# Stick-breaking sums in two reduced-precision passes with split operands instead of plain fp32 products

## The chip, the core and the metric

The program runs on one core of one Trainium2 chip. Its engines work side by side, each through its own queue in program order: TensorE (PE in the rows, PEld for its weight loads), VectorE (DVE), ScalarE (ACT), GpSimd (POOL) and SyncE (SP, which issues most DMAs). The metric is the time of one execution in device microseconds; less is better.

## The reference, cut to what matters

Two transformer-like blocks follow one another on 512 frames of width 1024. The change sits in one of the three mixers of the first block, a causal attention whose weights come from breaking a stick:

```
def stick_breaking_attention(q, k, v):        # 4 heads, head size 64, blocks of 128 frames
    for o in range(n):                        # nearest key block first
        z = einsum('bhnqd,bhnkd->bhnqk', qb[:, :, o:], kb[:, :, :n - o])
        log_rest = log_sigmoid(-z)            # diagonal block: masked
        after = einsum('bhnqj,js->bhnqs', log_rest, after_mat) + carry[:, :, o:, :, None]
        w = exp(log_sigmoid(z) + after)
        out = out.at[:, :, o:].add(einsum('bhnqk,bhnkd->bhnqd', w, vb[:, :, :n - o]))
        carry = carry.at[:, :, o:].add(sum(log_rest, axis=-1))
```

Beside it stand a chunked attention with relative positions (8 heads) and a short convolution. The three results are normalised in groups, multiplied by `w_out` and added to `x`; a feed-forward layer and the whole second block come after that.

## The kernel before

Everything is held transposed: 128 partitions by 512 frames. Large products run with both operands split in a high and a low part of the type fp32r, as three passes (`mm3`: low by high, high by low, high by high). The small products inside the attentions are plain fp32.

`block1` (line 606) issues the projections of the first block unit by unit. A unit is one 128x1024 slice of weights, w0, w1, ..., split into `w..h` on ACT and `w..l` on DVE; one projection takes eight groups of three passes. The order is the string `SEQ1`. The units that matter here are w16 to w19 (`qkb`, queries and keys of the last two pairs of chunked heads) and w20 to w23 (`g`, the convolution gates). Then comes the output projection `wo`: its first three row blocks (units w24 to w26) are gathered in the order `PRE1`, which is first the normalised output `ys0`, then `ys3, ys4, ys1, ys2`, then `ys6`, then `ys5, ys7`.

Beside this main stream run generators, in lanes of a merger (class `Merge`, line 138): the four stick-breaking heads (`sb_head`, lane `sb`, three at a time), the chunked heads (`ch_head`, lane `at`, four at a time), the convolution (`cv`) and small statistics (`ln`). When the program is built, the merger keeps a clock for each engine (`Clock`, line 64: a cost for each instruction and a time at which each tile will be ready). A generator yields the time from which it wants to go on; its next step is put in front of the next main product only when the planned time of PE has passed that time. Each engine then runs the instructions in the order in which they were written. So the table of costs and the yielded times set the order on all queues. Where `block1` asks for an output `ys[k]` that no generator has made yet, the merger runs side steps until it is there, with no main product between them.

One head of `sb_head` goes through the key blocks 3, 2, 1, 0; a block takes n = 128, 256, 384, 512 query columns. For each: a score product `z` on PE; `ab` (Abs, Exp, Ln) on ACT; `sp` (the softplus) on DVE; a triangular select on POOL; the product of the triangle `ntri` with `sp`, added into `z`; from the second block on the product of `nones` with the carried sum, n - 128 columns wide; then `w` = Exp on ACT, a select on POOL, and on DVE the new carry. At its end `osb` gathers the head's output, the group norm follows (`gsq` on ACT, `gst` on DVE and a power on POOL), and after each second head four transposes (`yT`) and a split into `ys..h` and `ys..l`. `ys1` needs head 3, and head 3 enters the lane when the first of heads 0 to 2 has left it.

One chunked head takes four blocks in turn: scores `sc`, `s` on DVE and ACT, its maximum `m` on DVE, Exp on ACT, transposes `pt`, a copy `pT`, the product `och` with the values, and a scaling on DVE (`sm`, `y`).

All calls go through the helper at line 134, so nearly every row of the profile carries that line; tiles tell the places apart.

Of the kernel before, what the change touches and what calls it, by code (L numbers as in the profile page):

```python
# [10 lines left out]
F32 = mybir.dt.float32  # L11
F32R = mybir.dt.float32r
# [3 lines left out]
AF = mybir.ActivationFunctionType  # L16
ALU = mybir.AluOpType
# [4 lines left out]
P = 128  # L22
T = 512
# [40 lines left out]
class Clock:  # L64
# [43 lines left out]
    def at(self, *aps):  # L108

        t = 0.0  # L110
        for x in aps:
            r = self.ready.get(x.tensor.name)
            if r:
                lo, hi = self.span(x)
                t = max([t] + [e[2] for e in r if e[0] < hi and e[1] > lo])
        return t
# [74 lines left out]
def body(tc, a):  # L191
    nc = tc.nc
    clk = Clock()
    V, S, G, PE = (Engine(clk, k, e) for k, e in (("V", nc.vector), ("S", nc.scalar), ("G", nc.gpsimd),
                                                  ("PE", nc.tensor)))
    at, room = clk.at, clk.room
    with ExitStack() as ctx:
        ctx.enter_context(tc.manual_schedule())

        def mkpool(stack, name, **k):  # L200
            return stack.enter_context(tc.tile_pool(name=name, bufs=1, **k))
# [25 lines left out]
        nones = cst.tile([P, P], F32, name="nones")  # L227
# [7 lines left out]
        ntri = cst.tile([P, P], F32, name="ntri")  # L235
# [7 lines left out]
        raws, parts = {}, {}  # L243
# [75 lines left out]
        wk = mkpool(ph, "wk")  # L319
# [4 lines left out]
        def t2(name, dt=F32):  # L324
            return wk.tile([P, T], dt, tag="t2", name=name, bufs=NT2)
# [73 lines left out]


        preload("natural_log_exp_and_others")
        mg = Merge(clk, at=4, sb=3, ln=1, cv=1, cg=1, ls=1, rw=1)
        run = mg.run
        y_tok = [t2(f"y{k}").rearrange("p (b d) -> p b d", b=NB) for k in range(KT)]
# [2 lines left out]
        def group_norm(*gs):  # L407

            st_ = []
            for g in gs:  # L410
                yg = y_tok[g // 2][:, :, (g % 2) * 64:(g % 2) * 64 + 64]
                sq = t2(f"gsq{g}")[:, :NB * 64].rearrange("p (b d) -> p b d", b=NB)
                S.activation(sq, yg, AF.Square)
                s_ = wk.tile([P, 3, NB], F32, tag="gst", name=f"gst{g}", bufs=6)
                st_.append((yg, sq, s_))
            yield at(*(x[1] for x in st_))
            for yg, sq, s_ in st_:
                V.tensor_reduce(s_[:, 0], sq, axis=AX.X, op=ALU.add)
                V.tensor_scalar(s_[:, 1], s_[:, 0], 1.0 / 64, EPS, ALU.mult, ALU.add)
                G.tensor_tensor(s_[:, 2], s_[:, 1], half[:, :NB], ALU.pow)  # L420
            yield at(*(x[2] for x in st_))
            for yg, sq, s_ in st_:
                V.tensor_tensor(yg, yg, s_[:, 2][:, :, None].to_broadcast([P, NB, 64]), ALU.mult)

        def y_transpose(k):
            pt = psd(f"yT{k}")
            for b in range(NB):
                PE.transpose(pt[:, b * P:(b + 1) * P], y_tok[k][:, b, :], ident)
            ys[k] = split(pt, f"ys{k}", scale=pc("out_norm", k))
# [3 lines left out]
        def sb_head(h):  # L433
            q, k = Q[f"qa{h // 2}"], Q[f"ka{h // 2}"]
            rows = slice((h % 2) * 64, (h % 2) * 64 + 64)
            wts = {}
            carry = None
            for kb in (3, 2, 1, 0):
                c0 = kb * P
                n = T - c0  # L440
                z = psd(f"z{h}{kb}")
                zz = z[:, c0:]
                PE.matmul(zz, k[rows, c0:c0 + P], q[rows, c0:], start=True, stop=True)
                ab = t2(f"ab{h}{kb}")
                S.activation(ab[:, c0:], zz, AF.Abs)
                S.activation(ab[:, c0:], ab[:, c0:], AF.Exp, scale=-1.0)
                S.activation(ab[:, c0:], ab[:, c0:], AF.Ln, bias=1.0)
                yield at(ab)
                sp = t2(f"sp{h}{kb}")
                V.scalar_tensor_tensor(sp[:, c0:], zz, 0.0, ab[:, c0:], ALU.max, ALU.add)  # L450

                G.affine_select(sp[:, c0:c0 + P], sp[:, c0:c0 + P], pattern=[[1, P]], base=0,
                                channel_multiplier=-1, compare_op=ALU.is_gt, fill=0.0)
                yield at(sp)
                PE.matmul(zz, ntri, sp[:, c0:], start=False, stop=True, skip_group_check=True)
                if carry is not None:
                    PE.matmul(z[:, c0 + P:], nones, carry[:, c0 + P:], start=False, stop=True,
                              skip_group_check=True)
                w = t2(f"w{h}{kb}")
                S.activation(w[:, c0:], zz, AF.Exp)  # L460
                G.affine_select(w[:, c0:c0 + P], w[:, c0:c0 + P], pattern=[[1, P]], base=0,
                                channel_multiplier=-1, compare_op=ALU.is_gt, fill=0.0)
                wts[kb] = w
                if kb:
                    if carry is not None:
                        V.tensor_tensor(sp[:, c0 + P:], sp[:, c0 + P:], carry[:, c0 + P:], ALU.add)
                    carry = sp
                yield None if kb else at(*wts.values())
            o = psd(f"osb{h}")
            for qb in range(NB):  # L470
                for kb in range(qb + 1):
                    PE.matmul(o[:, qb * 64:(qb + 1) * 64], wts[kb][:, qb * P:(qb + 1) * P],
                              va[kb // 2][:, kb % 2, h * 64:(h + 1) * 64], start=kb == 0, stop=kb == qb)
            V.tensor_copy(y_tok[h // 2][:, :, (h % 2) * 64:(h % 2) * 64 + 64],
                          o[:, :256].rearrange("p (b d) -> p b d", b=NB))
            yield at(y_tok[h // 2])
            yield from group_norm(h)
            if h % 2:
                yield at(y_tok[h // 2])
                y_transpose(h // 2)  # L480
# [125 lines left out]
        def block1():  # L606
# [3 lines left out]
            for x in SEQ1:  # L610
                if x == "a":
# [9 lines left out]
                    for h in range(4):  # L621
                        mg.spawn("sb", sb_head(h))
# [137 lines left out]
        for g in range(2):  # L760
            c = 64 * g
# [256 lines left out]
        wk = mkpool(ph, "wk2")  # L1018
# [523 lines left out]
```

## Time and profile before

| | us |
|---|---|
| median of three runs | 2438.34 (2435.8 to 2440.07) |
| profiled execution, device time | 2441.93 |
| its span, first to last instruction | 2440.1 |
| PE busy in the span | 2369.1 (97%) |
| DVE, ACT, POOL busy | 1759.5, 1036.5, 741.1 |

The span is read as one long stream of matmuls: PE is busy 97% of it. A busy PE need not be PE at its peak, since matmuls are pipelined and their ends are modelled; the starts of consecutive matmuls tell what one costs. The stick-breaking heads live between 132 and 250 us.

### The profile page before, as it was taken

To read this page: it belongs to the slowest core of one execution; us is meant where nothing else is said; L and a number is where in the kernel's file an instruction comes from. 1 tells how busy PE (TensorE), PEld (TensorE's weight loads), DVE (VectorE), ACT (ScalarE), POOL (GpSimd) and SP (SyncE) were. 2 spreads that over 40 slices of the span, in tenths; PEclk is the share of its full clock that TensorE was granted. 3 is DMA by queue.
4 is the path that set the end of the run, shared out by engine and by line. 5 is a ranking of instruction groups with operands and counts; after the bars stand their busy time and mean duration, and the time that the engine had idled before them with its cause. 6 is when DMAs were issued, how large, how long until landed. Compare 5 with 4: busy or idle time off the path is not lost.

```text
span 2440.1 us, 33936 instructions
## 1 busy us (share of the span) xinstructions
PE 2369.1 (97%) x13121; PEld 2113.9 (87%) x13121; DVE 1759.5 (72%) x3167; ACT 1036.5 (42%) x1557; POOL 741.1 (30%) x590
## 2 busy tenths in 40 slices
PE   9999999999999899999999999999998999999997
PEld 7777888888776667778889999999997999999997
DVE  4636644443357779755789899899997888888874
ACT  4454332222246456544334343455554333333333
POOL 2122011110116668401234455333322332323211
PEclk9999999999999999999999999999999999999998
DMA  4111222232211112222224788899998999999972
GB/s 169 59 53 35 89 88 104 86 104 89 93 61 64 58 53 69 88 97 97 87 100 171 279 320 308 303 329 345 344 328 271 360 357 366 350 362 356 372 292 86
DMA packets 141601, 466.14 MB, mean 191 GB/s; under 512 B 10624, under 2 KB 61952, under 8 KB 111744
## 3 DMA queue, kind: packets, MB, share of 16 engines
q1 hardware_dynamic: 51840, 279.47, 31.5%
q0 software_dynamic: 37184, 135.81, 15.6%
q10 hardware_dynamic: 52416, 48.70, 5.9%
q8 instruction: 103, 1.69, 0.3%
q14 instruction: 58, 0.48, 0.1%
HBM read 414.65 MB, written 49.28 MB: 190 GB/s over the span
## 4 chain that ended last, share of the span: by engine, by line
PE 71%; issue 11%; DVE 10%; ACT 3%; POOL 3%; DMA 2%; SPq 0%; DVEq 0%; POOLq 0%; ACTq 0%
PE acc L134 22%; PE u L134 13%; PE up L134 5%; PE gate L134 5%; PE pq L134 3%; DVE hot L134 2%; PE wo L134 2%; PE qkb L134 2%; PE gc L134 2%; DVE m L134 1%; PE co L134 1%; PE ao L134 1%; PE g L134 1%; PE ga L134 1%; PE gl L134 1%
## 5 line engine op out<-in xcount | busy, mean ns | idle before, releaser
L134 POOL TENSOR_TENSOR cy<-cy,cvt 128x511 f32<-128x511 f32 (+14 forms) x120 | 173.1, 1442 | 70.2 <-ACT cvt L134 59.0
L134 ACT ACTIVATE last<-u 128x384 f32<-128x384 f32 x128 | 63.0, 492 | 245.0 <-PE u L134 244.8
L1054 POOL DMA_INDIRECT last<-in_un,eid x64 | 80.1, 1252 | 168.3 <-DVE ea L134 131.9
L1054 POOL DMA_INDIRECT last<-in_vn,eid x64 | 70.6, 1104 | 184.1 <-DVE yt L134 174.2
L1054 POOL DMA_INDIRECT row<-in_un,eid x64 | 81.4, 1272 | 139.5 <-DVE ea L134 135.8
L1054 POOL DMA_INDIRECT row<-in_vn,eid x64 | 75.1, 1173 | 150.6 <-DVE yt L134 141.9
L134 ACT ACTIVATE stage<-gp 128x512 f32<-128x512 f32 x96 | 95.9, 1110 | 6.5 <-PE gp L134 6.5
L134 DVE TENSOR_TENSOR hot<-hot,ijb 128x1024 bf16<-128x1024 bf16 x144 | 91.0, 686 | 1.5
L134 PE MATMUL gp<-hot,hot 128*128 128x128 bf16 x1152 | 76.0, 221 | 14.2 <-ACT last L134 7.9
L134 PEld LDWEIGHTS <-hot 128*128 128x128 bf16 x1152 | 67.5, 98 | 24.5 <-DVE hot L134 20.4
L134 DVE SCALAR_TENSOR_TENSOR cyp<-u,par,cyp 128x511 f32<-128x511 f32 (+28 forms) x116 | 85.3, 736 | 2.4
L134 DVE CUSTOM_DVE_ANT_0 last<-last,h2tok 128x1024 f32<-128x1024 f32 x64 | 77.3, 1214 | 9.4 <-DMA last<-in_un,eid 9.2
L134 DVE SCALAR_TENSOR_TENSOR yt<-row,ea,yt 128x1024 f32<-128x1024 f32 x64 | 81.9, 1279 | 0.1
L134 DVE SCALAR_TENSOR_TENSOR yt<-last,ea,yt 128x1024 f32<-128x1024 f32 x63 | 80.6, 1279 | 1.7 <-DMA last<-in_vn,eid 1.7
L134 DVE CUSTOM_DVE_ANT_0 row<-row,h2tok 128x1024 f32<-128x1024 f32 x64 | 77.1, 1213 | 3.8 <-DMA row<-in_un,eid 3.7
L134 ACT ACTIVATE cvt<-u,par 128x511 f32<-128x511 f32 (+14 forms) x120 | 78.9, 701 | 0.0
L134 DVE TENSOR_TENSOR wv<-last,goct 128x384 f32<-128x384 f32 x128 | 70.6, 552 | 5.9 <-DMA goct<-g_dr 5.9
L134 DVE TENSOR_TENSOR hot<-iota,ijb 128x1024 bf16<-128x1024 bf16 x96 | 61.7, 683 | 0.0
L134 DVE TENSOR_TENSOR su<-up,n2r 128x512 f32<-128x512 f32 x22 | 15.2, 691 | 51.4 <-PE up L134 51.4
L134 PEld LDWEIGHTS o<-v,pT 128*128 128x128 f32 x224 | 29.5, 200 | 18.1 <-DVE pT L134 9.7
L134 PE MATMUL o<-v,pT 128*128 128x64 f32 x224 | 32.0, 285 | 9.6 <-DVE pT L134 6.4
L134 DVE MAX8 stop__8676<-skc 128x8 f32<-128x128 f32 x128 | 36.8, 287 | 5.5 <-ACT skc L134 3.2
(6459 smaller groups left out, 8474.0 us busy)
## 6 DMA issues: line engine op xcount, KB each, us to landing
raw<-in_w SPq DMA_DIRECT2D x89, 1024.0 KB
raw<-in_u SPq DMA_DIRECT2D x64, 1024.0 KB
raw<-in_v SPq DMA_DIRECT2D x64, 1024.0 KB
g_dr<-stage ACTq DMA_DIRECT2D x24, 1024.0 KB
goct<-g_dr SPq DMA_DIRECT2D x60, 384.0 KB
a_dr<-last ACTq DMA_DIRECT2D x14, 1536.0 KB
last<-a_dr SPq DMA_DIRECT2D x56, 384.0 KB
goct<-g_dr POOLq DMA_DIRECT2D x4, 384.0 KB
```

Source lines behind the costliest of these rows:

```text
L134: return f(*args, **kw)
L1054: nc.gpsimd.indirect_dma_start(row_buf(n), None, t, bass.IndirectOffsetOnAxis(ap=eid[:, n % P:n % P + 1], axis=0))
```

## The change

For each product with 256 columns or more the softplus tile (or the carry) is split into a high part, rounded to fp32r by ACT (`sh`), and a low part, the difference, by DVE (`sl`). The triangle and the ones are copied to fp32r once (`ntrir`, `nonesr`). The product is then two passes, low and high, instead of one plain fp32 product. Narrower products stay as they were. Of a head's seven products five are split: 256, 384 and 512 columns with the triangle, 256 and 384 with the ones. The yield in front of the products now waits for the parts.

```
         preload("natural_log_exp_and_others")
+        ntrir = wk.tile([P, P], F32R, name="ntrir")
+        V.tensor_copy(ntrir, ntri)
+        nonesr = wk.tile([P, P], F32R, name="nonesr")
+        V.tensor_copy(nonesr, nones)
...
-                yield at(sp)
-                PE.matmul(zz, ntri, sp[:, c0:], start=False, stop=True, skip_group_check=True)
-                if carry is not None:
-                    PE.matmul(z[:, c0 + P:], nones, carry[:, c0 + P:], start=False, stop=True,
-                              skip_group_check=True)
+
+                jobs = [(ntri, ntrir, sp, c0)] + ([(nones, nonesr, carry, c0 + P)] if carry is not None else [])
+                parts = []
+                for w32, wr, x, c in jobs:
+                    if T - c < 256:
+                        parts.append((w32, x, c))
+                        continue
+                    xh, xl = t2(f"sh{h}{kb}{c}", F32R), t2(f"sl{h}{kb}{c}", F32R)
+                    S.activation(xh[:, c:], x[:, c:], AF.Copy)
+                    V.tensor_tensor(xl[:, c:], x[:, c:], xh[:, c:].bitcast(F32), ALU.subtract)
+                    parts += [(wr, xl, c), (wr, xh, c)]
+                yield at(*(x[1] for x in parts))
+                for w_, x, c in parts:
+                    PE.matmul(z[:, c:], w_, x[:, c:], start=False, stop=True, skip_group_check=True)
+                jobs = parts = None
```

The new instructions and the new yield change the planned times, and with them the order on PE, DVE, ACT and POOL from the unit w17 to the end of the gathering with w26; SP's order and all that follows stay as they were.

On PE before, from the last pass of the last `g` projection (w23) on: the last transposes of two chunked heads, `yT` of a finished pair, and four products later the output projection begins.

```order
L134 MATMUL g_2034<-attn_normh,w23h 128x512
L134 MATMUL pt_2156<-ident,s_2101 128x128 x4
L134 MATMUL yT_2163<-ident,y_106 128x128 x4
L134 MATMUL pt_2172<-ident,s_2107 128x128 x4
L134 MATMUL och_2179<-vb_317,pT_2161 128x64
L134 MATMUL och_2179<-vb_319,pT_2161 128x64
L134 MATMUL och_2179<-vb_321,pT_2161 128x64
L134 MATMUL och_2179<-vb_323,pT_2161 128x64
L134 MATMUL wo_2153<-ys0l,w24h 128x512
```

On PE in the changed kernel, right behind the same last pass of w23: chunked heads in their first and second blocks, and at the end of these rows the score product of the first key block of stick-breaking head 3 (`z_1957`).

```order
L134 MATMUL pt_1876<-ident,s_1804 128x128 x2
L134 MATMUL sc_1888<-qk_1498,qk_1418 128x128
L134 MATMUL sc_1896<-qk_1498,qk_1418 128x128
L134 MATMUL och_1912<-vb_321,pT_1855 128x64
L134 MATMUL och_1912<-vb_323,pT_1855 128x64
L134 MATMUL sc_1917<-qk_1331,qk_1263 128x384
L134 MATMUL och_1923<-vb_321,pT_1879 128x64
L134 MATMUL och_1923<-vb_323,pT_1879 128x64
L134 MATMUL sc_1928<-qk_1331,qk_1263 128x384
L134 MATMUL pt_1940<-ident,s_1890 128x128
L134 MATMUL pt_1944<-ident,s_1898 128x128
L134 MATMUL z_1957<-qa_951,ka_1079 128x128
```

All of head 3 and about three quarters of the last four chunked heads have moved behind the last projection. The stretch ends on PE with the last products of head 3, its transposes, and the first pass of the gathering with `ys3`:

```order
L134 MATMUL osb_2331<-va_183,w_2183 128x64
L134 MATMUL osb_2331<-va_184,w_2069 128x64
L134 MATMUL yT_2347<-ident,y_114 128x128 x4
L134 MATMUL yT_2360<-ident,y_110 128x128 x4
L134 MATMUL wo_1873<-ys3l,w24h 128x512
L134 MATMUL wo_1873<-ys3h,w24l 128x512
```

From `pt_1876` to the second `yT` PE has 104 such rows, nine of them wide passes (`wo` from `ys0`), in which head 3 is carried from its first key block to its group norm; before, nearly all of these small products stood between passes of `qkb` and `g`.

On ACT in the changed kernel, in the same stretch, around the high part of head 3's second key block (`sh_2135`), whose softplus `sp_2132` DVE makes and POOL masks:

```order
L134 ACTIVATE ab_2096<-ab_2096 128x256 x2
L134 ACTIVATE gsq_2100<-y_116 128x256
L134 ACTIVATE gsq_2103<-y_116 128x256
L134 ACTIVATE s_2080,sm_1895<-s_2080,m_2083 128x384
L134 ACTIVATE pT_2119<-pt_2114 128x512
L134 ACTIVATE s_2088,sm_1627<-s_2088,m_2091 128x512
L134 ACTIVATE sh_2135<-sp_2132 128x256
```

and on DVE there:

```order
L134 COPY pT_2127<-pt_2123 128x384
L134 SCALAR_TENSOR_TENSOR sp_2132<-z_2094,ab_2096 128x256
L134 TENSOR_TENSOR sl_2136<-sp_2132,sh_2135 128x256
L134 RECIPROCAL sm_1887<-sm_1887 128x1
L134 TENSOR_SCALAR y_114<-och_2139,sm_1887 128x64
```

Both instructions are new: DVE now has the subtraction, which needs ACT's copy, in front of the chunked heads' steps.

## Rows read from the trace of the kernel before

**Rows 1.** The page: the chain that ended last, shares of the span.
```profile
PE 71%; issue 11%; DVE 10%; ACT 3%; POOL 3%; DMA 2%; SPq 0%; DVEq 0%; POOLq 0%; ACTq 0%
```
**Rows 2.** Busy time by stretch: us, engines (x instructions), granted clock, DMA share, GB/s.
```profile
145.74:240.39 94.65, 94.58 (x501) 70.66 (x500) 54.62 (x134) 47.65 (x106) 23.43 (x36) 0.95 0.12 44
240.39:263.19 22.80, 22.20 (x118) 18.22 (x117) 15.26 (x36) 9.26 (x17) 5.98 (x6) 1.00 0.00 1
190.00:212.00 22.00, 22.00 (x108) 16.44 (x107) 11.67 (x29) 9.49 (x23) 5.96 (x8) 0.77 0.00 1
```
**Rows 3.** Timeline of PE: start us, us, operation; plain fp32 sums, then split passes.
```profile
168.13 1.02 PE L134 MATMUL z<-sp,ntri 128*128 128x512 f32 x2
168.99 0.81 PE L134 MATMUL z<-sp,nones 128*128 128x384 f32 x2
...
151.74 0.39 PE L134 MATMUL qkb<-attn_normh,w18h 128*128 128x512 f32 x1
...
152.43 0.39 PE L134 MATMUL qkb<-attn_normh,w18h 128*128 128x512 f32 x1
```
**Rows 4.** Timeline of PE: small products of both attentions, under wide ones.
```profile
229.57 2.34 PE L134 MATMUL osb<-va,w 128*128 128x64 f32 x20
235.31 1.45 PE L134 MATMUL och<-vb,pT 128*128 128x64 f32 x12
240.76 0.66 PE L134 MATMUL pt<-ident,s 128*128 128x128 f32 x4
241.25 0.60 PE L134 MATMUL yT<-ident,y 128*128 128x128 f32 x4
```
**Rows 5.** DVE from 190 to 262 us by shape: count | busy us, mean ns | idle before.
```profile
L134 DVE TENSOR_TENSOR y<-y,gst 128x256 f32<-128x256 f32 x10 | 4.1, 416 | 0.4 <-POOL gst L134 0.3
L134 DVE TENSOR_REDUCE gst<-gsq 128x4 f32<-128x256 f32 x9 | 3.7, 410 | 0.0
L134 DVE SCALAR_TENSOR_TENSOR s<-sc,qkr,tb 128x256 f32<-128x256 f32 x8 | 3.7, 481 | 2.8 <-PE sc L134 2.8
L134 DVE TENSOR_SCALAR y<-och,sm 128x64 f32<-128x64 f32 x12 | 3.4, 284 | 2.6 <-PE och L134 1.7
L134 DVE TENSOR_REDUCE m<-s 128x1 f32<-128x512 f32 x4 | 2.6, 679 | 0.2 <-ACT s L134 0.2
L134 DVE COPY pT<-pt 128x384 f32<-128x384 f32 x4 | 2.2, 552 | 1.3 <-PE pt L134 1.3
L134 DVE RECIPROCAL sm<-sm 128x1 f32<-128x1 f32 x12 | 1.8, 152 | 0.0
L134 DVE TENSOR_TENSOR gbc<-g,n1r 128x512 f32<-128x512 f32 x2 | 1.4, 692 | 4.8 <-PE g L134 4.8
L134 DVE SCALAR_TENSOR_TENSOR ys5l<-yT,par,ys5h 128x512 fp32r<-128x512 f32 x1 | 0.8, 751 | 0.4 <-ACT ys5h L134 0.4
```
**Rows 6.** ACT and POOL from 131 to 262 us by shape, columns as in rows 5.
```profile
L134 ACT ACTIVATE s<-s,m 128x512 f32<-128x512 f32 x4 | 2.8, 713 | 2.1 <-DVE m L134 2.1
L134 ACT ACTIVATE w<-z 128x512 f32<-128x512 f32 x4 | 2.4, 597 | 6.0 <-PE z L134 6.0
L134 POOL TENSOR_TENSOR gst<-gst,half 128x4 f32<-128x4 f32 x12 | 12.0, 1007 | 27.2 <-DVE gst L134 26.4 <-DVE sm L134 0.8
L134 POOL TENSOR_SCALAR_AFFINE_SELECT sp<-sp 128x128 f32<-128x128 f32 x16 | 4.9, 312 | 36.3 <-DVE sp L134 29.9 <-DVE qkv L134 5.3 <-DVE sm L134 0.9
```
**Rows 7.** Timeline of DVE: its wait at the start, and two neighbours with no wait.
```profile
5.94 0.69 DVE L134 TENSOR_TENSOR w0l<-raw,w0h 128x512 fp32r<-128x512 f32 x1 [4.66 <-ACT w0h L134]
...
240.16 0.41 DVE L134 TENSOR_TENSOR y<-y,gst 128x256 f32<-128x256 f32 x1
240.50 0.41 DVE L134 TENSOR_REDUCE gst<-gsq 128x4 f32<-128x256 f32 x1
```
**Rows 8.** Timeline of POOL and DVE: a DVE product of two tiles beside a power on POOL.
```profile
185.31 1.01 POOL L134 TENSOR_TENSOR gst<-gst,half 128x4 f32<-128x4 f32 x1 [1.80 <-DVE gst L134]
...
185.53 0.41 DVE L134 TENSOR_TENSOR y<-y,gst 128x256 f32<-128x256 f32 x1
```

## The prediction

> **What bounds the kernel now.** The chain of work that ended last comes first: it is mostly PE [rows 1]. Then the windows over the part of the first block that the change reaches. From 145.74 us, where the order of the two kernels first differs on PE, to 240.39 us, the last `g` pass, PE is busy 94.58 of 94.65 us while DVE and ACT work about half of it; from there to 263.19 us, the end of the three gathered `wo` blocks, it is busy 22.20 of 22.80 [rows 2]. The heads' ACT and DVE steps are covered by wide passes: PE hardly waits. So two questions decide: how much PE work goes, and whether PE still has wide work to do while the heads' chains run.
>
> **What is removed and added on PE.** A plain 512-column product takes 0.86 us from start to start (168.13 to 168.99) [rows 3], 1.68 ns a column. Three split passes take 0.69 us (151.74 to 152.43), 0.23 each, 0.45 ns a column; two of them, 0.90 ns. Each head has 256 + 384 + 512 + 256 + 384 = 1792 such columns, four heads 7168, so 7168 x 0.78 ns = 5.6 us of PE go. The page "TensorE: Matmul & The Clock Gate" of the Trainium skill (Back-to-back issue gap) gives some 131 ns for a sustained 512-column matmul; by that figure two passes would cost 0.26 us and the saving would be 8.3 us. This trace says 229 ns for the very kind of pass, and I use that.
>
> **What is added elsewhere.** 20 copies on ACT and 20 subtractions on DVE. ACT copies of 256 to 512 columns cost up to 0.60 us each (as `w` at 512) [rows 6], DVE's 0.42 (256 columns, `y` by `gst`) to 0.69 us (512, `gbc`) [rows 5]; about 9 and 11 us in all. Three quarters belong to heads 0 to 2, which still run beside the projections. I cost those at nothing: 49 groups of three passes (49 x 0.69 = 34 us) still stand between them on PE, and the planner puts a head's products behind the time at which it expects the parts. The nearest case is the first, head 0's 256 columns: one more group (0.69 us) and four small `qkst` now stand ahead of it, while the copy and the subtraction add some 1.0 us to what it waits for. Where such cover is gone, a step costs that 1.0 to 1.5 us, at most 15 times. The two casts of the constants at the start fall in 4.66 us in which DVE waits for ACT [rows 7]: nothing.
>
> **What is moved.** This is the large term. The longer planned steps delay the heads in the planner's account, so the projections go first and the heads pile up behind them. After the last `g` pass the changed order has all of head 3 and most of the last four chunked heads, and `wo` cannot go on past `ys0` before `ys1`, that is head 3, is done. I call the stretch from that pass to the first `wo` pass from `ys3` the tail.
>
> PE's work in the tail, at the prices of covered work: 38 `och` products at 0.23 us (12 records, six products, 1.38 us from 235.31 to 236.69, 1.45 busy) 9; 64 transposes at 0.12 (four from 240.76 to 241.25) 8; `osb` 2.3; nine `wo` passes 2.1 [rows 3, 4]; head 3's products 2; its scores and the chunked heads' at 0.9 us for 512 columns, many of them in pairs, 9; starts after a change of operands 1.5. Sum 34 us.
>
> DVE's queue in the tail has 119 instructions, from the convolution's first product to `ys1`'s low part. By kind: 14 `y` x 0.28 = 4.0; 14 reciprocals x 0.15 = 2.1; 12 group-norm products x 0.42 = 5.0; 12 `gst` sums x 0.41 = 4.9 and their 12 scalings x 0.17 = 2.0; 10 `s` x 0.48 = 4.8; 12 maxima of 128 to 512 columns (0.68 at 512), 6.3; 4 `pT` x 0.55 = 2.2; 6 `ys` low parts x 0.75 = 4.5; the convolution and the low part of w26, five instructions of 0.5 to 0.75 and one of 1.2, 4.6; 17 others from 0.28 to 0.69, 7.6 [rows 5]. Sum 48; a next instruction that depends on nothing starts some 0.07 us before the last one ends (240.16 + 0.41 against 240.50 [rows 7]), which takes back 5: 43 us if DVE never waits.
>
> It will wait, since each queue runs in order. After head 3's second softplus DVE stands before `sl` until POOL has masked (0.31) and ACT has copied, and ACT has a transposed copy and a 512-column Exp of chunked heads before that copy (about 0.6 + 0.7 + 0.4) [rows 6]: 2.7 us. At the third block a power on POOL (1.01) comes ahead of the select: 1.5. At the fourth 1.1. `ys4`'s low part waits for ACT behind a `w`, three steps of `ab` and two more: 3.4. The last products, Exp (0.60), select (0.31) and `osb` (2.3) before DVE's copy: 4.8, of which DVE has 2.3 of other work: 2.5. Then `ys5`, sum, power (1.01), product, `yT` in line: 2.7. Two waits for `och` 1.4. Sum 15, with 0.5 before the first instruction 59 us.
>
> So in the tail PE idles 59 - 34 = 25 us, and the change costs 25 - 5.6 = 19 us before the clock. **Clock.** After a stretch of small products the granted clock was 0.77 on average from 190 to 212 us [rows 2], between its levels 1.2 and 2.4 GHz, worth up to 0.23 x 22 = 5 us of PE time. With wide passes there instead I expect much of that dip to go (-3); in the tail PE has far thinner work, so I expect the lower level in it: the PE steps on the path, some 8 us of the sum, may double, and the first `wo` passes run slow (+5). Net +2: 21 to 22 us. That is bounded by -5 (the dip goes, none comes) and by +13 (8 us doubled, 5 at the start of `wo`, no dip saved).
>
> **A rule against it.** In the trace a DVE product of two SBUF tiles took its usual 0.41 us at 185.53 inside a power on POOL (185.31, 1.01 us) [rows 8], so I add nothing for POOL. The page "SBUF — State Buffer" of the Trainium skill (SBUF: two separate sides) says that a DVE instruction with two SBUF inputs and a GpSimd instruction that reads SBUF share a port pair under an exclusive lock, the loser waiting for the whole instruction. By that rule that product should have waited 0.8 us; this row disagrees.
>
> **Rivals.**
> - **The tail is short, and the kernel is faster.** If chains of five heads interleave without the waits, DVE's own 43 us, lapped a little by PE, are near PE's 34. The point from which it decides: the tail must be under 34 + 5.6 = 40 us. Fully covered, the time is 5.6 us lower, 2433 (with the dip gone 2428). Against it: DVE alone needs 43 us and the last chain behind it. 3%.
> - **Only the queue, few waits.** A tail of 43 + 6 (the last chain: products, Exp, select, `osb`, sum, power) = 49 us: 15 - 5.6 = +9, time 2448. For it: some waits may lap. 20%.
> - **A slow tail.** The clock stays low through the tail and chains between ACT, PE and POOL add more than my short list: 59 + 9 and 5 more at `wo`: +33, time 2471. For it: the dip after 190 us came with PE nominally 100% busy. 20%.
> - **GpSimd's powers hold DVE up.** By a lock such as the rule above states, up to eleven powers of 1.01 us in the tail [rows 6] would each keep DVE waiting: +11 on the forecast, 2471; the row of 185.53 us speaks against it [rows 8]. 4%.
> - **The split is not cheaper.** If these passes cost as much as plain ones the 5.6 us stay: 2466. The row for `qkb` speaks against it [rows 3]. 3%.
>
> **How the numbers follow.** The profiled execution took 2441.93 us, its span 2440.1; with +22 the span becomes 2462 and the device time 2464. The median of the runs is 3.6 us lower, so the forecast is 2438.3 + 22 = 2460 us, with 50%. 0.2% is about what a measurement of this kernel can tell from no change, 4.9 us. Of the short-queue rival a small part ends within that, of the forecast nothing. Faster 3%, same 3%, slower 94%. The range leaves out the fast rival and the ends of the two 20% cases: 2446 to 2475.
>
> **What would show it.** In the profile after: `z` passes with `ntrir` at 0.23 us per 512 columns; the last `g` pass near 208 us in place of 240.39 (240.4 less the 34 us moved behind it, of which 6 stood there before, less three quarters of the 5.6); then some 55 to 68 us in which PE idles by 20 or more, its idle time put down to DVE and ACT (tiles `pT`, `s`, `sl`, `y`), while DVE is busy above 70%; the end of the w26 block near 285 us instead of 263 (208 + 59 + 63 passes at 0.23, and the clock); everything after it shifted as a whole. A tail of 40 us or less would overturn the forecast; PE idling before 208 us for `sl` would show the cover of heads 0 to 2 to be thinner than I said.

## The result and the profile after

| | before | after |
|---|---|---|
| median of six runs each, us | 2439.2 (2435.8 to 2444.78) | 2471.79 (2463.09 to 2477.59) |
| profiled execution, its span | 2441.93, 2440.1 | 2475.03, 2473.3 |
| last `g` pass starts | 240.39 | 208.22 |
| first `wo` pass from `ys3` starts | 246.9 | 281.45 |
| first pass of the next unit, w27 | 263.2 | 297.7 |

The ratio is 1.0134 (95% interval 1.012 to 1.0147): the change costs 32.6 us. All of it arises ahead of w27, which starts 34.5 us later; the 2175 us after that take 1.2 us less than before. About 1.7 us of the 34.5 are there before the order differs (the last pass of w15 starts at 133.8 us, before at 132.1). They begin at the start, where the second half of the first weights came later: its low part was made at 8.86 instead of 7.61 us, and over the kernels below that start lies between 7.5 and 10.0. Executions of one kernel differ with the clock that they were granted: the six of after take 2463 to 2478 us, the profiled one being among the three above 2475 (mean clock 0.976 to 0.978, the others 0.979 to 0.981), and the split in the order of before (below) has three near 2453 us (0.986 to 0.987) and three near 2464 (0.980 to 0.981), while each profile shows one execution.

Windows of after, to be laid beside [rows 2]: us, then busy us of PE, PEld, DVE, ACT and POOL with their instructions, granted clock, DMA share, GB/s.

```profile
145.74:208.22 62.48, 62.48 (x346) 50.09 (x346) 35.45 (x71) 32.70 (x66) 16.38 (x26) 1.00 0.20 68
208.22:281.45 73.23, 57.52 (x217) 41.21 (x216) 42.01 (x119) 32.31 (x78) 14.37 (x20) 0.61 0.00 1
281.45:297.65 16.20, 16.20 (x65) 13.16 (x64) 2.05 (x3) 2.81 (x3) 0.00 (x0) 0.89 0.00 1
```

The first line is denser than before: PE never idles and the clock stays up; the dip after 190 us [rows 2] is gone. That need not be the change's doing: two kernels below that keep the products and nearly the order of before (copies alone, and subtractions that wait for nothing) show 1.00 from 180 to 220 us as well. The second line is the tail that the reordering makes. Its clock, 0.61, is a mixture of the two levels; which stretch has which is shown below. VectorE's waits in the tail are these (engine, tile, what it waited for: us in total, times, longest):

```profile
DVE y L134 <- PE och L134: 5.6, 4, 2.5
DVE y L134 <- PE osb L134: 4.8, 1, 4.8
DVE sl L134 <- ACT sh L134: 3.5, 3, 1.5
DVE s L134 <- PE sc L134: 3.2, 5, 0.9
DVE pT L134 <- PE pt L134: 3.2, 1, 3.2
DVE ys5l L134 <- ACT ys5h L134: 2.0, 1, 2.0
DVE ys4l L134 <- ACT ys4h L134: 1.9, 1, 1.9
DVE ys6l L134 <- ACT ys6h L134: 1.3, 1, 1.3
DVE y L134 <- POOL gst L134: 1.2, 1, 1.2
DVE y L134 <- PE cvt L134: 1.1, 1, 1.1
DVE gst L134 <- ACT gsq L134: 0.5, 1, 0.5
DVE hc L134 <- PE g L134: 0.2, 1, 0.2
```

and TensorE's these:

```profile
PE yT L134 <- DVE y L134: 6.1, 3, 3.8
PE z L134 <- DVE sl L134: 4.2, 2, 2.3
PE pt L134 <- ACT s L134: 2.4, 1, 2.4
PE och L134 <- DVE pT L134: 1.8, 1, 1.8
PE osb L134 <- POOL w L134: 1.2, 1, 1.2
```

Each waits for the other, but VectorE for TensorE (18.1 us) longer than TensorE for VectorE (12.1): the prediction had only 3.9 us of the first, and the third part of the experiments deals with it. The passes themselves are as cheap as forecast (timeline of PE: start, duration, operation):

```profile
185.68 0.39 PE L134 MATMUL z<-sl,ntrir 128*128 128x512 f32 x1
185.91 0.40 PE L134 MATMUL z<-sh,ntrir 128*128 128x512 f32 x1
186.14 0.34 PE L134 MATMUL z<-sl,nonesr 128*128 128x384 f32 x1
186.32 0.33 PE L134 MATMUL z<-sh,nonesr 128*128 128x384 f32 x1
```

From start to start 0.23 us for 512 columns, so 0.46 for the pair in place of 0.86 for the plain product [rows 3].

### The profile page after: what moved, and what is told of

Same layout as the page of the kernel before. It is cut to its first block, busy times and chain, and to the rows that moved or that the text cites. A ratio compares the mean times of both kernels' runs of the same rounds, so it can differ in the third digit from the quotient of the medians.

```text
span 2473.3 us, 33968 instructions
## 1 busy us (share of the span) xinstructions
PE 2384.2 (96%) x13121; PEld 2125.7 (86%) x13121; DVE 1771.2 (72%) x3189; ACT 1047.7 (42%) x1577; POOL 741.0 (30%) x590
## 4 chain that ended last, share of the span: by engine, by line
PE 66%; issue 15%; DVE 11%; POOL 4%; ACT 3%; DMA 2%; SPq 0%; POOLq 0%; DVEq 0%; ACTq 0%
PE acc L134 22%; PE u L134 9%; PE up L134 5%; PE gate L134 5%; PE pq L134 3%; PE wo L134 2%; PE qkb L134 2%; DVE hot L134 2%; PE gc L134 2%; PE ga L134 2%; DVE m L134 1%; PE g L134 1%; POOL last L1068 1%; PE co L134 1%; POOL row L1068 1%
## 5 line engine op out<-in xcount | busy, mean ns | idle before, releaser
L134 DVE CUSTOM_DVE_ANT_0 last<-last,h2tok 128x1024 f32<-128x1024 f32 x64 | 77.3, 1216 | 11.0 <-DMA last<-in_un,eid 11.0
L134 DVE CUSTOM_DVE_ANT_0 row<-row,h2tok 128x1024 f32<-128x1024 f32 x64 | 77.3, 1216 | 5.5 <-DMA row<-in_un,eid 5.4
```

Of the source, the lines that this page charges most:

```text
L134: return f(*args, **kw)
```

## The experiments

Twelve kernels, in three questions. Each was timed beside runs of the kernel before on its own chip, whose medians lay between 2436.9 and 2441.1 us.

### Is it the order or the split?

**Plain products in the order of after.** The planner is charged for the copies, subtractions and passes, but none is issued; the old products stand at their places.

```
-                    S.activation(xh[:, c:], x[:, c:], AF.Copy)
-                    V.tensor_tensor(xl[:, c:], x[:, c:], xh[:, c:].bitcast(F32), ALU.subtract)
+                    clk.op("S", "activation", (xh[:, c:], x[:, c:]), {})
+                    clk.op("V", "tensor_tensor", (xl[:, c:], x[:, c:], xh[:, c:]), {})
...
+                for w32, wr, x, c in jobs:
+                    nc.tensor.matmul(z[:, c:], w32, x[:, c:], start=False, stop=True, skip_group_check=True)
```

> Plain fp32 products without copies and subtractions, but the planner is charged for the split, so the queues keep the changed kernel's order. Theory (the order costs): as slow as the changed kernel, about 2468 to 2478 us: its 5.6 us are lost on PE, some 5 us of waits for sl in the tail are saved. Rival (the split costs): back near 2440 to 2450 us.

Measured: 2468.46 us, ratio 1.0125 (1.0108 to 1.0143). The reordering alone costs what the whole change costs.

**The split in the order of before.** The new instructions are issued past the planner, which is charged for the plain products and keeps `yield at(sp)`.

```
-                    S.activation(xh[:, c:], x[:, c:], AF.Copy)
-                    V.tensor_tensor(xl[:, c:], x[:, c:], xh[:, c:].bitcast(F32), ALU.subtract)
+                    nc.scalar.activation(xh[:, c:], x[:, c:], AF.Copy)
+                    nc.vector.tensor_tensor(xl[:, c:], x[:, c:], xh[:, c:].bitcast(F32), ALU.subtract)
...
-                yield at(*(x[1] for x in parts))
+                yield at(sp)
+                for w32, wr, x, c in jobs:
+                    clk.op("PE", "matmul", (z[:, c:], w32, x[:, c:]), {})
```

> The split copies, subtractions and two-pass products are all there, but the planner is told of the plain products alone and the yield waits for sp as before, so every queue keeps the order of the kernel before with only the new instructions put in. If the order is the cause of the loss (theory): the 33 us are gone and the 5.6 us of PE time come back, 2431 to 2437 us, PE idle after the last g pass as before. If the split itself costs (rival: the copies and subtractions stand in front of the heads' chains on ACT and DVE): still slower than before, 2445 us or more, with PE waiting for sl between the projections.

Measured: 2458.47 us, ratio 1.009 (1.0069 to 1.0112). So the split costs in the old order too, 22 us, although its passes are 5.6 us cheaper. TensorE's waits from 130 to 282 us, where the kernel before has one of 0.6 us:

```profile
PE z L473 <- DVE sl L467: 7.5, 5, 2.1
PE yT L134 <- DVE sm L134: 1.6, 1, 1.6
PE pt L134 <- ACT s L134: 1.4, 2, 1.2
PE krb L134 <- POOL qkr L134: 1.4, 1, 1.4
```

**Only the yield put back.** The planner is charged for everything, but the generator goes on once `sp` is planned ready (shown against after).

```
-                yield at(*(x[1] for x in parts))
+                yield at(sp)
```

> The changed kernel with one line different: the yield ahead of the products waits for sp as before, not for the parts; the planner is still charged for copies, subtractions and passes. The tail then has 64 PE rows in place of 105, with 9 of head products in place of 16. Theory (the length of the tail decides): a tail of some 40 us, total 2445 to 2458 us. Rival (it is the charge on the planned ACT and DVE clocks, not the yield): as the changed kernel, 2468 to 2476 us.

Measured: 2458.06 us, ratio 1.008 (1.0065 to 1.0096); the last `g` pass stands at 226.5 us, the tail is 39.6 us long. The yield therefore carries 11 to 13 us of the 32.6 (by the medians and by the ratios): it puts the heads one step later, and a longer tail behind the last projection is the price.

### Why does the split cost where the order is kept?

The edits of this part are shown against the split in the order of before; those of the copies alone and of the subtractions that wait for nothing against the first kernel of this part, whose products are plain.

**Copies and subtractions that nobody reads**, at their places in the order of before, with the plain products reading `sp` itself.

```
-                for w_, x, c in parts:
-                    nc.tensor.matmul(z[:, c:], w_, x[:, c:], start=False, stop=True, skip_group_check=True)
+                for w32, wr, x, c in jobs:
+                    nc.tensor.matmul(z[:, c:], w32, x[:, c:], start=False, stop=True, skip_group_check=True)
```

> The order of before with the 20 copies and 20 subtractions at their places, whose results nobody reads: the products are plain and read the softplus tile itself. Theory (what costs is that TensorE waits for the subtraction): 2435 to 2443, within 0.3% of before. Rival (the engines' time and their queues cost): 2448 or more, most of the 21.6 us that the split costs in this order.

Measured: 2449.02 us, ratio 1.0038 (1.0025 to 1.0051). My theory was that only TensorE's waiting for the parts costs; it fell, since here TensorE waits for none. VectorE's queue shows why (timeline of DVE in this run: start, duration, operation, and in brackets the idle time before it and what ended it):

```profile
163.16 1.23 DVE L134 TENSOR_TENSOR w21l<-raw,w21h 128x1024 fp32r<-128x1024 f32 x1 [2.40 <-ACT w21h L134]
164.31 0.55 DVE L134 SCALAR_TENSOR_TENSOR sp<-z,ab 128x384 f32<-128x384 f32 x1
165.81 0.90 DVE L467 TENSOR_TENSOR sl<-sp,sh 128x384 fp32r<-128x384 f32 x2 [0.95 <-ACT sh L466]
166.62 0.16 DVE L134 TENSOR_SCALAR qkv<-qkst 128x8 f32<-128x8 f32 x1
```

Behind `sp` VectorE stands still for 0.95 us, until POOL has masked the tile and ACT has copied it. The `qkv` behind it, a step of another generator, starts 1.76 us after `sp` has ended, and `krb` on TensorE, which needs it through POOL, waits 2.05 us at 168.66. From VectorE's list of waits in this run (us in total, times, longest):

```profile
DVE sl L467 <- ACT sh L466: 16.0, 12, 2.8
```

It stands so at twelve places. The split in the old order has 16.6 us of it, and after has 16.8.

**The copies alone**, without subtractions, in the order of before.

```
                     nc.scalar.activation(xh[:, c:], x[:, c:], AF.Copy)
-                    nc.vector.tensor_tensor(xl[:, c:], x[:, c:], xh[:, c:].bitcast(F32), ALU.subtract)
```

> The order of before with the 20 copies on ACT alone, read by nobody: no subtraction, products plain. Copies and subtractions together cost 8 us there (2449.0 against 2441.1). Theory (the heads' chains pass ACT between the scores and their Exp, and the softplus through ACT's Abs, Exp and Ln, so a copy of 0.4 to 0.7 us at ACT's queue holds them): more than half of it stays, 2445 or more. Rival (VectorE's subtraction, which waits for the copy and holds VectorE's queue meanwhile, is what costs): 2438 to 2443.

Measured: 2440.22 us, ratio 1.0002 (0.9992 to 1.0011). ACT's 20 copies are free; my theory, that ACT's queue would be held, fell.

**Subtractions that wait for nothing.** The same place and size, reading the Ln result that VectorE has just read.

```
-                    nc.vector.tensor_tensor(xl[:, c:], x[:, c:], xh[:, c:].bitcast(F32), ALU.subtract)
+                    nc.vector.tensor_tensor(xl[:, c:], ab[:, c:], ab[:, c:], ALU.subtract)
```

> As the run with dead copies and subtractions and plain products in the order of before (2449.0, 8 us above before; with the copies alone 2440.2), at the same places, but each subtraction reads the tile that VectorE's instruction just before has read (the Ln result, from itself), so that it waits neither for POOL's selection nor for the copy: 20 subtractions of VectorE's time without the 16 us for which VectorE stood still. Theory 1 (the standing costs): 2437 to 2443. Theory 2 (VectorE's busy time, 20 subtractions of 0.42 to 0.6 us, costs): 2446 to 2450.

Measured: 2442.54 us, ratio 1.0019 (1.001 to 1.0027). That lies at the upper end of the range of theory 1, and half of the 0.38% remains, so each theory has about half. In the old order the price of the split is thus a ladder with a run for each rung: copies 0.0%, subtractions as busy time 0.2%, their waiting in VectorE's queue another 0.2% (the two intervals just overlap, so this rung is the least certain), and the passes that wait for them another 0.5%, though those passes save 5.6 us. In that last rung TensorE's waits (7.5 us) are only a part: the mean clock of the whole run is also lower there, 0.9835 against 0.9877 with dead copies and subtractions (means of six runs each). Worked out from that, an estimate, up to 0.0042 x 2450 = 10 us of the rung come with the clock. "TensorE: Matmul & The Clock Gate" in the Trainium skill (Architectural detail) says that ACT and DVE are strict FIFO; VectorE's rows above agree.

**The passes later.** As the split in the old order, but the products come 1.2 us after `sp` in the planner's account; beside it plain products in that very order.

```
-                yield at(sp)
+                yield at(sp) + 1.2
```

> As the split in the order of before (its run: 2458, with TensorE waiting for the subtractions for 0.9 to 2.1 us each), but the planner lets each head's products come up only 1.2 us after the softplus tile is ready, so that about one other step of TensorE stands between the subtraction and the passes; 14 rows of TensorE stand between the last pass of g and the first pass of wo on ys3. Theory (the split costs by its latency on the path, nothing else): the waits of 0.9 to 2.1 us go, 5.6 us of products are saved, 2428 to 2440 us. Rival (the copies and subtractions fill ACT's and VectorE's queues and hold others up): 2446 or more, with TensorE idle before steps other than these products.

> The control of the one before: plain fp32 products without copies, in that same order (products 1.2 us later by the plan). It gives what the order alone is worth. Theory: 2434 to 2444, and the split version is below it by the 5.6 us that its products save; rival: the split version is above it by 5 or more.

Measured: split 2463.74 us, ratio 1.0096 (1.0082 to 1.0109); plain 2450.16, ratio 1.004 (1.0028 to 1.0053). TensorE hardly waits for `sl` any more (0.7 us once), and yet the split is 13.6 us behind its control: the theory that it costs by its latency alone fell, the waiting has gone to other generators. TensorE's waits in the split version:

```profile
PE wo L134 <- DVE w26l L134: 3.4, 1, 3.4
PE pt L134 <- ACT s L134: 3.1, 4, 1.3
PE och L134 <- DVE pT L134: 2.9, 1, 2.9
PE sc L134 <- DVE qk L134: 1.8, 1, 1.8
```

and in the plain one, where these two are all:

```profile
PE wo L134 <- DVE w26l L134: 3.4, 1, 3.4
PE yT L134 <- DVE y L134: 1.1, 2, 0.9
```

The windows add the clock: from 160 to 180 us the split version has it at 0.66, the plain one at 1.00.

**The subtraction later too**, 0.6 us after `sp` by the plan, so that other steps of VectorE come first; the passes 1.6 us after it.

```
+                if subs:
+                    yield ready + 0.6
+                for xl, x, xh, c in subs:
+                    nc.vector.tensor_tensor(xl[:, c:], x[:, c:], xh[:, c:].bitcast(F32), ALU.subtract)
+                yield ready + (1.6 if subs else 0.0)
```

> The split with the planner charged for plain products, close to the order of before (22 rows of TensorE stand between the last pass of g and the first pass of wo on ys3, as 21 before); the copies stay where they are, but the planner lets a subtraction come 0.6 us after the softplus tile and its passes 1.6 us after it, so that 4 to 38 rows of VectorE stand between the two instead of none. In the runs with the subtraction right behind, VectorE stood still for 16 to 17 us for the 20 copies. Theory (it is this standing in VectorE's queue, not the subtractions' 8 us of busy time, that costs): the waits of VectorE for sh fall below 6 us, and the kernel takes 2432 to 2444 us, no slower than before by more than 0.2%. Rival (VectorE's time itself, or the heads made later by 1 to 1.6 us a step): 2448 or more.

Measured: 2476.93 us, ratio 1.0158 (1.0144 to 1.0172), as slow as any kernel here. VectorE's waits for `sh` were gone from its list, as expected, but TensorE paid instead:

```profile
PE z L479 <- DVE sl L474: 16.0, 5, 7.4
PE yT L134 <- DVE y L134: 3.1, 1, 3.1
...
DVE w21l L134 <- ACT w21h L134: 5.4, 1, 5.4
```

In the step of 7.4 us the subtraction stands in VectorE's queue right behind `w21l`, work of the main stream that itself waits 5.4 us for ACT's `w21h`. This order has no control with plain products, so what the later steps alone cost is not known. Putting an instruction later in one queue without telling the planner here moved the standing from one engine to the next. In none of the orders tried does the split gain.

### Why is the tail 73 us long?

I had reckoned 59. The candidate was the clock: most of the tail ran at the lower level, 1.2 GHz. The test is to keep TensorE busy with passes of zeros and see whether the tail shortens although there is more to do. Two such runs spread them over the whole tail, one puts them at its head alone.

**Fillers over the whole tail**, two passes (112 in all), then one (56), behind each step.

```
+            def fill():
+                for _ in range(2):
+                    nc.tensor.matmul(pre[2], zeror, us[0][0][:, :T], start=not begun[0], stop=not begun[0],
+                                     skip_group_check=True)
```

> The changed kernel with 112 extra passes of 512 columns with zero weights, two behind each PE step of the tail, which add zeros to an accumulator: they keep PE at work while it would wait (112 x 0.23 = 26 us at the full clock). If the lower clock stretched the tail from the 59 us of my sum to the 73 measured: granted clock in the tail near 1.0 in place of 0.61, tail 60 to 66 us, total 2460 to 2467 us. If the chains between ACT, DVE and POOL set the 73 us whatever the clock: tail 73 us or more, up to 85 with the extra passes in the way, total 2472 to 2484 us.

> The changed kernel with one pass of zeros over 512 columns (0.23 us) behind each step of TensorE between the last pass of g and the wo products, 56 in all, in place of 112. With 112 the granted clock in the stretch was 1.00 up to 270, but TensorE was full up to 256, with fillers for some 26 us of it. Theory (at the lower clock TensorE's steps double and become the stretch's limit): with half the fillers the clock stays above 0.8 in the stretch and it takes 62 to 69 us in place of 73.2, 2460 to 2468 in all. Rival (the clock does not set the stretch, VectorE's queue and its waits do): 73 us or more whatever the clock, 2471 or more.

Measured: 2478.18 us, ratio 1.0159 (1.0142 to 1.0177), and 2477.57, ratio 1.0145 (1.0123 to 1.0166). Tails of 77.3 and 72.1 us at mean clocks of 0.93 and 0.84: by the totals expected, both go against the clock (the second tail lies between its two ranges). But with 112 fillers TensorE was busy 39.33 of 40.00 us from 218 to 258 at 1.00, and with 56 it was busy 34.42 of 35.32 from 218.37 at 0.90, so the fillers' own time may have taken what the clock gave. The two runs don't settle it; the next one was made so that no filler stands in that part.

**Fillers at the head alone**, 26 of them, where TensorE waits 4.1 us for VectorE's queue anyway.

```
+                filled[0] += 1
+                for _ in range(2 if filled[0] < 11 else 6 if filled[0] == 11 else 0):
+                    nc.tensor.matmul(pre[2], zeror, us[0][0][:, :T], start=not begun[0], stop=not begun[0],
+                                     skip_group_check=True)
```

> The changed kernel with 26 passes of zeros (512 columns, 0.23 us each) behind the first eleven steps of TensorE after the last pass of g (two each, six behind the last), and none later: they lie in the stretch 208 to 218, where TensorE waits 4.1 us for VectorE's queue anyway and where its clock falls; the 124 TensorE instructions from 218 to 253 stay as they are. In the changed kernel these took 35.2 us at a mean clock of 0.63; in the plain products with the same order 27.1 us at 0.85. Theory (the lower clock is what makes this part longer than the 20 us or so of VectorE's queue beside it): with the hole before it filled the clock starts the part at 1.00 and the part takes 24 to 29 us, the whole stretch 61 to 68, the kernel 2459 to 2467. Rival 1 (the clock falls again at once, since VectorE's waits thin the part itself): part 33 us or more, 2469 or more. Rival 2 (clock up, part no shorter): then its length was never TensorE's.

Measured: 2463.62 us, ratio 1.01 (1.0086 to 1.0114): 8 us less than after, with 6 us of useless passes added, and within the range of the theory. The tail falls into three parts: a head up to the `och` that starts the long run of small products, that run up to the transposes for `ys7`, and the end up to `wo` from `ys3`. In after:

```profile
208.22:218.00 9.78, 5.56 (x24) 3.07 (x23) 9.03 (x25) 4.59 (x13) 1.70 (x2) 0.77 0.01 2
218.00:253.18 35.18, 33.84 (x124) 23.78 (x124) 21.40 (x65) 17.90 (x46) 6.40 (x10) 0.63 0.00 1
253.18:281.45 28.27, 18.11 (x70) 14.36 (x71) 11.58 (x31) 9.82 (x19) 6.27 (x9) 0.52 0.00 0
```

With the fillers at the head:

```profile
208.99:220.52 11.53, 11.53 (x51) 7.35 (x50) 10.71 (x31) 4.65 (x14) 3.46 (x4) 1.00 0.01 1
220.52:246.06 25.54, 22.32 (x124) 15.38 (x123) 19.49 (x59) 17.03 (x46) 4.63 (x8) 1.00 0.00 1
246.06:274.34 28.28, 18.15 (x71) 14.39 (x71) 11.58 (x31) 9.80 (x19) 6.26 (x9) 0.54 0.00 0
```

With plain products in the order of after:

```profile
211.12:220.95 9.83, 5.56 (x24) 3.07 (x22) 9.01 (x25) 4.57 (x13) 1.70 (x2) 0.72 0.01 2
220.95:248.05 27.10, 25.76 (x123) 18.48 (x124) 21.05 (x64) 17.12 (x45) 6.39 (x10) 0.85 0.00 1
248.05:276.15 28.10, 20.68 (x71) 14.41 (x71) 9.58 (x27) 8.15 (x15) 6.13 (x9) 0.53 0.00 0
```

The middle part holds the same steps in all three, but for the product of one key block, which is split in the first two, and six instructions of VectorE that fall into the longer head with the fillers. At a clock of 0.63 it takes 35.2 us, at 0.85 27.1, at 1.00 25.5. The head costs 1.75 us more with the fillers, the middle 9.64 less, the end is the same to 0.01 us: 7.9 in sum. The medians of the two kernels differ by 8.2 us; the two profiled executions differ by 11.4, part of it behind the tail. So TensorE at half clock is the limit of the middle part in after. That answers the second filler run too: its middle had the higher clock and 34 passes more to do. The plain products' tail is 65.0 us, 8.2 less than the split's, nearly all of it in the middle part; the last section shows why that can't be put down to the split.

## Why the prediction was right in sign and low by 12 us

I forecast 2460 us, in a range from 2446 to 2475, and 94% for slower; it is 2471.8. By its steps:

- **The saving on PE: right.** 0.40 us for each 512 columns, as reckoned from [rows 3]. The rival that the split is not cheaper is out.
- **The order: right.** The last `g` pass was forecast near 208 us and starts at 208.22; the plain products in that order show that the order alone makes the loss.
- **The cover of heads 0 to 2 at nothing: right for this order, but for a reason that I had only half.** PE is busy 62.48 of 62.48 us there. In the order of before the same split costs 22 us, its copies and subtractions without the passes 0.38%. What covers them is that the planner was charged for them and put other wide passes ahead. I had asked only how long TensorE would wait for the parts; the larger question was who stands behind a waiting subtraction in VectorE's queue.
- **VectorE's queue in the tail: right.** 43 us forecast, 42.01 busy. Its waits for ACT and POOL, forecast as 2.7 + 1.5 + 1.1 + 3.4 + 2.7 = 11.4, came to 10.4, worked out from its list of waits (3.5 + 2.0 + 1.9 + 1.3 + 1.2 + 0.5), though not in the same places: `sl` waited less than reckoned at its first step (0.84 us in the timeline, against 2.7).
- **The step that failed: TensorE's part of the tail.** Of VectorE's waits for TensorE I had counted 1.4 for `och` and 2.5 at the last products; they were 18.1 (5.6 + 4.8 + 3.2 + 3.2 + 1.1 + 0.2). This excess, 14.2 us, is as large as the gap between 59 and 73.2: VectorE's own time and its waits for ACT and POOL came 1.0 us each below the forecast, and 2.7 us of the tail are neither in its busy time nor in its list, of which I had 0.5. TensorE's own part, 34 us in my sum, was 57.52. I had priced TensorE's steps as in covered work [rows 4], called 8 us of them "on the path" and put +5 on the lower clock, +2 net. But at the lower level TensorE's steps from 218 to 240 us took all of the time, so the path ran through nearly all of them and not through 8 us. `osb` shows the price itself, 4.53 us against 2.34 before [rows 4], and so do two groups of four transposes (timeline of PE):

```profile
270.36 4.53 PE L134 MATMUL osb<-va,w 128*128 128x64 f32 x20 [1.18 <-POOL w L134]
275.83 1.09 PE L134 MATMUL yT<-ident,y 128*128 128x128 f32 x4 [0.94 <-DVE y L134]
280.71 1.09 PE L134 MATMUL yT<-ident,y 128*128 128x128 f32 x4 [3.80 <-DVE y L134]
```

  The run with fillers at the head shows 7.9 us of the 14.2 (9.6 in the middle part, less the 1.75 by which the head grew); of the rest 2.2 lie in `osb` and 1.0 in those transposes of 1.09 instead of 0.60 (both worked out from rows, not tried), and 3.1 stay open.
- **The bounds of the clock term** reached to +13 where +2 was taken, and the slow tail stood among the rivals with 2471 us and 20%: its time is nearly the one measured, but that is in part luck. Its low clock through the tail is shown. Yet it put 9 of its 14 us on longer chains between ACT, PE and POOL, where ACT's and POOL's part ran as forecast and the excess was TensorE's alone, and 5 us on slow passes at `wo`, which took 16.2 us for some 14.5 at 0.23 each.
- **The other rivals.** The short tail is out (73 us against 40), the mere queue too (49). GpSimd's powers did not hold VectorE: its 42.01 us busy for 119 instructions leave no room for 11 us more, and VectorE's list of waits has only 1.2 us on POOL.
- **The dip of [rows 2].** I took -3 for its going. It may not belong to the kernel: the mean clock of that profiled execution was 0.985, and of the 63 executions of the kernel before that were timed beside the twelve kernels 59 had 0.987 or more.
- **The signs.** The price of the passes, the place of the last `g` pass and the tiles for which PE waits (`y`, `sl`, `s`, `pT`) came as named. The sizes did not: the tail was 73.2 us (55 to 68 named), PE idled 15.7 us in it (20 or more), DVE was busy 57% of it (above 70%), and the w26 block ended at 297.65 us (near 285). PE idled less than I thought because its steps took longer.

## What to carry to other kernels

When a change feeds an automatic order, price the order first: here the same instructions cost 22 or 33 us by place, and every order tried lost more than the 5.6 us saved. For a new instruction in an in-order queue, list what stands behind it while it waits; on VectorE the wait for its operand cost about as much as its busy time, 0.2% each. And where a stretch turns from wide passes to small products, price TensorE's steps there at the lower clock, and ask whether it thereby becomes the limit.

## What the runs showed of the chip that was not expected

- **A hole of 4 us in TensorE's work was paid for over the next 26.** From 208 to 218 us PE was busy 5.78 of 10 us. The granted clock fell within that hole and then stood at 0.50 up to 244 us, although the records show PE busy without a gap; it rose behind nine wide `wo` passes. With the hole filled it stood at 1.00 up to 246.

```profile
208.00:218.00 10.00, 5.78 (x25) 3.25 (x24) 9.25 (x25) 4.81 (x13) 1.70 (x2) 0.77 0.01 2
218.00:230.00 12.00, 12.00 (x39) 8.75 (x40) 9.60 (x30) 5.17 (x15) 3.54 (x5) 0.50 0.00 1
230.00:240.00 10.00, 10.00 (x27) 6.30 (x26) 5.13 (x13) 4.05 (x11) 0.29 (x1) 0.50 0.00 0
240.00:253.18 13.18, 11.84 (x60) 8.73 (x59) 6.67 (x23) 8.68 (x21) 2.57 (x4) 0.84 0.00 1
```

  The fillers closed the hole and also put wide passes among the small products, and no run separates the two. A hole is not needed for a fall: in the kernel before the clock fell near 197 us, after a run of small products (from 192.9 us on) with PE busy throughout, and came back near 207.

- **The same steps did not always get the same clock.** In the same order the mean clock of the tail was 0.69 with plain products and 0.61 with the split ones, and the tail 65.0 and 73.2 us. In both it fell in the same hole. It rose at 229 us, 18 us behind the last `g` pass, in the plain run, and at 244, 36 us behind it, in after. Up to the step at which it rose in the plain run both had issued the same products since that pass, and the first split product of the tail comes at 247.53 us, when the clock was already up. So the split products of the tail are not the reason. Whether the difference belongs to the kernels or to the two executions profiled was not tried.
